# An encoder layer on one core: gates and RG-LRU projection in 2x2 blocks, products that run on in one PSUM bank, and a mix that is turned

## The chip, the core and the metric

The kernel runs on one core of a Trainium2 chip. A core has five engines that run side by side and meet at semaphores: TensorE (PE in the profile; its weight loads are shown apart as PEld), VectorE (DVE), ScalarE (ACT), GpSimd (POOL) and SyncE (SP), which here only issues transfers. TensorE writes its products into PSUM, 128 partitions of 8 banks of 512 fp32 numbers; DVE and ACT read them from there. Everything else lies in SBUF, and inputs, outputs and scratch lie in DRAM.

The metric is the time of one execution on the device in microseconds (us), lower is better. It is the median of several runs.

## What is computed

One layer of a hybrid encoder over 512 tokens of width 1024, in fp32:

```python
h = rmsnorm(x, mix_norm)
rx, ry, qkv, z, ba, gates = split(h @ w_in)          # w_in: 1024 x 9248
y_rnn = rglru_branch(rx, ry, ...) @ w_rnn_proj       # 1536 x 1024
y_dn  = deltanet_branch(qkv, z, ba, ...) @ w_dn_proj # 1024 x 1024
g_rnn, g_dn = split(sigmoid(gates))                  # 2 x 1024 columns
x = x + (g_rnn * y_rnn + g_dn * y_dn) @ w_out
gt, up = split(rmsnorm(x, ffn_norm) @ w_gate_up)     # 1024 x 2*2816
x = x + (silu(gt) * up) @ w_down
return rmsnorm(x, final_norm)
```

The RG-LRU branch is a short convolution, two gates and a linear scan along the tokens in both directions, times gelu(ry). The DeltaNet branch has 8 heads of 128 and works on chunks of tokens in both directions; its output is normalised per head and multiplied by silu(z).

## The kernel before

**Precision.** Each fp32 operand of a large product is split in two parts: hi, a copy rounded to the type that TensorE takes in one pass (a cast on ACT), and lo = value - hi (a subtraction on DVE, in a few places on POOL or by a DMA that accumulates). A product is hi*hi + hi*lo + lo*hi, three matmuls for each k-tile of 128.

**Two forms of product.** The plain form, `mm3`, keeps a weight tile of 128 output columns in TensorE and streams 512 tokens: the result has channels on the partitions. The block form (`products`, used for z; the same scheme by hand in gate/up, w_out and w_down) cuts tokens, rows and columns in halves and computes the 2x2 blocks with seven products in place of eight, from sums of blocks (names "1" to "7"). Sums of weight blocks are made by DMAs that add to what lies in SBUF (on POOL's queue, `accum_op`); sums of the normed input h are made once in `h_combos` and kept in DRAM (`xqd`).

**Stages.** Norm and transposes of x; four groups of three RG-LRU blocks (`rg_front` for rx, `rg_out` for ry); the z columns (`zset`); four groups of two DeltaNet heads (`dn_front`, `dn_mats`, `dn_inverse`, `dn_state`, `dn_out`); the gates, the RG-LRU projection (`rnn_part`) and the DeltaNet projection (`dn_part`); the mix times w_out; the second norm; gate/up, 22 tiles of 128 columns, of which 20 in block form; w_down; the last norm.

Before the change the gates and both projections are in the plain form. `rnn_part(i, n)` multiplies half of the 1536 rows by 128 columns; `rnn_gate(n)` and `dn_gate(n)` make 128 columns of a gate; `dn_part(h0, nh, n)` multiplies four heads by 128 columns and adds the gated result to the mix. The mix has channels on the partitions (`mixs`), as w_out's product needs it; `out_q(j)` makes the block sums of 256 of its columns.

**What sets the order.** The functions only record operations. `ORDER` lists all of them by number, over all engines; `Plan.emit` issues them in that order, and each engine works through its own queue in it. `HOMES` gives each SBUF and PSUM tile (pools t2, t4, ps) its place, and a new user of a place waits for the last user of it. All eight PSUM banks are places of this kind. Since every operation is issued through one recorder, all have the same line, L516, in the profile; they are told apart by the names of their tiles (t, ps, hh, hl, na and so on), engines and shapes.

Of the kernel before, what the change touches and what calls it, by code (L numbers as in the profile page):

```python
# [464 lines left out]
"""  # L465
LASTK = 3
DSPLIT = 4
GATES = (0, 2, 4, 6, 16)
RG_GROUPS = [[0, 1, 2], [3, 4, 5], [6, 7, 8], [9, 10, 11]]

# [51 lines left out]
def trunk(ctx: ExitStack, tc: tile.TileContext, x, mix_norm, w_in, rg_conv_w, rg_conv_b, rg_wa, rg_ba, rg_wx, rg_bx,  # L522
# [431 lines left out]


    mix = [None] * KD

    def k_proj(wv, n, k0, kts, acts):
        po = mmb()
        hi, lo = weights(wv[:, k0:k0 + kts, n * P:(n + 1) * P], kts)  # L960
# [964 lines left out]
```

## Time and profile before

| | us |
|---|---|
| median of 3 runs | 1039.06 |
| lowest and highest | 1038.81, 1039.10 |
| span of the profiled execution | 1038.7 |
| matmul instructions in it | 6675 |
| mean granted TensorE clock | 0.997 |
| HBM read and written | 133.18 MB, 18.91 MB |

The profile is of one execution. "Busy" is the time in which an engine had an instruction at work. Matmuls are pipelined, so a record lasts longer than the distance to the next start. The chain of work goes back from the last instruction, at each step to what released it. Rows of groups give the operation, its output and input tiles, partitions x elements, the count, busy us and mean ns of one, and then the idle time of the engine just before them with what ended it. Rows of stretches give the busy time of the engines asked for, with their counts, then the granted clock, the share of the 16 DMA engines' time and GB/s.

### The profile page before, as it was taken

How to read it: one execution, taken by the hardware profiler on the slowest of the kernel's cores; microseconds unless marked ns; L12 is line 12 of the kernel's file. 1: busy time of each engine (PE TensorE's matmuls, PEld its weight loads, DVE VectorE, ACT ScalarE, POOL GpSimd, SP SyncE). 2: the span in 40 equal slices, each digit the busy share in tenths (PEclk: the TensorE clock that was granted, in tenths of full speed). 3: DMA queues.
4: the chain of work that ended last, by engine and by line, in shares of the span. 5: the costliest groups of instructions: out<-in, count | busy, mean ns of one | idle time of the engine just before them, and what ended most of it. 6: DMA issues, size and time to landing. Idle time of an engine off the chain costs nothing.

```text
span 1038.7 us, 18051 instructions
## 1 busy us (share of the span) xinstructions
PE 1028.2 (99%) x6675; PEld 902.0 (87%) x6675; DVE 906.1 (87%) x1699; ACT 730.5 (70%) x1331; POOL 91.1 (9%) x145
## 2 busy tenths in 40 slices
PE   9999999999999999999999999999999999999997
PEld 8988888888888888798888888889999999998886
DVE  6899998959896589659859979999999998999998
ACT  8699999998457766798897565578444544455674
POOL 6000000112000111142212000000000000000000
PEclk9999999999999999999999999999999999999999
DMA  9952442325644125979985636976555332256532
GB/s 300 308 159 85 144 120 85 90 56 127 183 96 122 50 80 151 267 177 219 232 222 134 183 114 213 304 217 200 166 174 173 118 102 82 83 203 198 180 109 81
DMA packets 185512, 163.75 MB, mean 158 GB/s; under 512 B 7728, under 2 KB 156352, under 8 KB 185424
## 3 DMA queue, kind: packets, MB, share of 16 engines
q1 hardware_dynamic: 178752, 144.37, 46.0%
q0 software_dynamic: 5344, 14.82, 7.9%
q10 hardware_dynamic: 1328, 3.42, 0.9%
q8 instruction: 52, 0.85, 0.3%
q14 instruction: 36, 0.29, 0.1%
HBM read 133.18 MB, written 18.91 MB: 146 GB/s over the span
## 4 chain that ended last, share of the span: by engine, by line
PE 98%; ACT 1%; DMA 0%; issue 0%; DVE 0%; ACTq 0%; DVEq 0%
PE ps L516 98%; ACT t L516 1%; DMA t<-in_w_in_dram 0%; ACTq L516 0%; DVE t L516 0%; ACT L516 0%; DVE na L516 0%; DVEq L1920 0%; DVE so L516 0%; ACT so L516 0%; ACT rst L516 0%; ACT warm L516 0%; DVE rin L516 0%
## 5 line engine op out<-in xcount | busy, mean ns | idle before, releaser
L516 PE MATMUL ps<-t,t 128*128 128x512 f32 (+3 forms) x3039 | 536.0, 322 | 2.5 <-issue 1.6
L516 DVE TENSOR_TENSOR t<-t,t 128x512 fp32r<-128x512 f32 (+19 forms) x807 | 506.3, 658 | 27.8 <-ACT t L516 13.4
L516 PEld LDWEIGHTS ps<-t,t 128*128 128x128 f32 (+1 forms) x3039 | 430.6, 180 | 58.2 <-issue 2.7
L516 PE MATMUL ps<-hh,t 128*128 128x512 f32 (+2 forms) x1680 | 456.5, 347 | 0.0
L516 ACT CAST t<-t 128x512 fp32r<-128x512 f32 (+2 forms) x400 | 298.0, 780 | 158.9 <-DVE t L516 60.5
L516 PEld LDWEIGHTS ps<-hh,t 128*128 128x128 f32 (+1 forms) x1680 | 298.1, 189 | 38.2 <-ACT t L516 0.2
L516 PE MATMUL ps<-hl,t 128*128 128x512 f32 (+2 forms) x848 | 278.6, 347 | 0.0
L516 PEld LDWEIGHTS ps<-hl,t 128*128 128x128 f32 (+1 forms) x848 | 158.4, 189 | 19.5 <-issue 0.2
L516 ACT ACT_TABLE_LOAD x73 | 93.7, 1283 | 12.0 <-DVE so L516 5.1
L516 DVE SCALAR_TENSOR_TENSOR t<-ps,par,t 128x511 f32<-128x511 f32 (+1 forms) x108 | 79.3, 744 | 14.7 <-ACT t L516 13.7
L516 ACT COPY t<-ps 128x512 f32<-128x512 f32 (+3 forms) x108 | 44.3, 429 | 52.7 <-PE ps L516 51.4
L516 ACT ACTIVATE t<-t 128x128 f32<-128x128 f32 (+5 forms) x114 | 72.6, 647 | 9.8 <-DVE t L516 8.0
L516 DVE TENSOR_TENSOR t<-ps,t 128x256 f32<-128x256 f32 (+1 forms) x106 | 50.3, 486 | 11.4 <-PE ps L516 8.7
L516 DVE TENSOR_TENSOR t<-t 128x512 f32<-128x512 f32 (+1 forms) x81 | 51.0, 636 | 0.9 <-DMA t<-in_w_out_dram 0.6
L516 ACT ACTIVATE t<-ps,par 128x512 f32<-128x512 f32 x68 | 45.8, 707 | 7.4 <-PE ps L516 7.2
L516 POOL TENSOR_SCALAR_AFFINE_SELECT t<-t 128x512 f32<-128x512 f32 x32 | 25.6, 807 | 218.5 <-DMA t<-gcr 107.5
L516 PE MATMUL ps<-t,na 128*128 128x128 f32 (+2 forms) x640 | 42.9, 232 | 0.0
L516 PEld LDWEIGHTS ps<-t,na 128*128 128x128 f32 (+2 forms) x640 | 39.6, 145 | 3.8 <-issue 1.4
L516 ACT ACTIVATE t<-ps 128x512 f32<-128x512 f32 (+1 forms) x58 | 28.7, 508 | 15.5 <-PE ps L516 15.0
L516 PE MATMUL ps<-ident,t 128*128 128x128 f32 (+1 forms) x200 | 32.4, 276 | 0.3 <-DVE t L516 0.3
L516 POOL DMA_DIRECT2D t<-t x20 | 18.1, 938 | 146.4 <-ACT t L516 131.3
L516 DVE SCALAR_TENSOR_TENSOR t<-ps,negc,t 128x128 f32<-128x128 f32 x48 | 13.7, 344 | 19.0 <-PE ps L516 18.9
(151 smaller groups left out, 612.4 us busy)
## 6 DMA issues: line engine op xcount, KB each, us to landing
t<-in_w_in_dram SPq DMA_DIRECT2D x70, 512.0 KB, 5.2
t<-in_w_gate_up_dram SPq DMA_DIRECT2D x44, 512.0 KB, 5.0
t<-in_w_down_dram SPq DMA_DIRECT2D x22, 512.0 KB, 4.9
t<-t POOLq DMA_DIRECT2D x20, 512.0 KB, 6.0
t<-in_w_down_dram SPq DMA_DIRECT2D x33, 256.0 KB, 3.8
t<-in_w_out_dram SPq DMA_DIRECT2D x12, 512.0 KB, 6.0
t<-in_w_rnn_proj_dram SPq DMA_DIRECT2D x16, 384.0 KB, 3.6
sums<-t SPq DMA_DIRECT2D x11, 512.0 KB, 4.1
```

Source lines behind the costliest of these rows:

```text
L516: self.plan.ops.append((self.eng, {x.tensor.name for x in aps}, outs, lambda: real(*a, **kw)))
```

## The change

- The gates (two sets of 1024 columns) and the RG-LRU projection are now computed with tokens on the partitions, as 2x2 blocks with seven products (`merged`), in place of the plain form. A set has seven products of n blocks, n = 2 for the gates and 3 for the projection. For the gates the blocks of h come from `h_get2`; for the projection `mixed` makes them from the RG-LRU output, which is no longer split in hi and lo by `rg_out`.
- In `merged` several products run on in the same PSUM banks: bank pair bx takes products 6, 7, 4 (and 1 in the projection), bz takes 5 and 3, bw takes 2 (and 1 in the gates). The signs of some sums are turned for that. Between two products the sum so far is copied out.
- The DeltaNet projection has tokens on the partitions too (`dn_half`, four heads at a time, 512 columns), with the same number of matmuls as before.
- The mix is kept with tokens on the partitions (`mixt`) and turned by 32 transposes ahead of w_out, whose blocks are now taken in the order 2, 3, 0, 1.
- In gate/up the products 1, 6, 7, 4 run on in one bank and 5 and 3 in another, so that a tile takes three banks in place of four and two operations fewer on DVE, with two copies more on ACT.
- `WAYS` says for each product how its lo part is made: V on DVE, P on POOL, D by an accumulating DMA.
- `ORDER` and `HOMES` are made anew; ORDER has 9344 operations in place of 9257. In its new form the second gate set stands ahead of the RG-LRU projection, the first one behind it. Ahead of the last group's output transposes 20 matmuls of the DeltaNet projection stand behind the last state matmul (27 before). Of the last `dn_half`, 64 matmuls stand behind the point from which the last two heads are needed; then 29 transposes of the turn, then the first product with w_out.

```diff
-DSPLIT = 4
-GATES = (0, 2, 4, 6, 16)
+OUT_J = (2, 3, 0, 1)
+GATES = (0, 6, 12, 18, 28)
+WAYS = {"z": dict(zip("1234567", "PPDVVVD")), "r": dict(zip("1234567", "VVVVVVV")), "g": dict(zip("1234567", "VVDVVVD")),
+        "h": dict(zip("1234567", "VVDVVVD"))}
...
-        V.tensor_tensor(gy, h_, gy, ALU.mult)
-        y = four(F32R)
-        split(gy, y)
-        yr[b] = y
+        if b % 2 == 0:
+            yr[b // 2] = four()
+        V.tensor_tensor(yr[b // 2][:, b % 2, :], h_, gy, ALU.mult)
...
+    def block(wv, c0, rows, way, name, j, run):
...
+        if name == "1":
+            src = four()
+            for k in range(2):
+                Q.dma_start(src[:, k, :], part(0, 0)[:, k, :])
+        elif name in "237":
+            src = new(t4, (P, 2, 512), "t4", 1)
+            for k in range(2 if name == "2" else 1):
+                ks = slice(k, k + 1) if name == "2" else slice(0, 2)
+                Q.dma_start(src[:, ks, :], part(*{"2": (1, 0), "3": (1, 1), "7": (0, 1)}[name])[:, ks, :])
+            if name == "7":
+                G.dma_start(src, part(1, 1), accum_op=ALU.add)
+        else:
+            if name == "5":
+                run[j] = four()
+                Q.dma_start(run[j], part(0, 0))
+            src = run[j]
+            G.dma_start(src, part(*{"5": (0, 1), "6": (1, 1), "4": (1, 0)}[name]), accum_op=ALU.add)
+        hi, lo = four(F32R), four(F32R)
+        if way == "D":
+            A.copy(hi, src)
+            A.activation(lo, f(hi), AF.Copy, scale=-1.0)
+            G.dma_start(lo, src, accum_op=ALU.add)
...
+        else:
+            parts_of(src, hi, lo)
+        return hi, lo
+
+    def block_mm(po, w, x_, start, stop, add=False):
+        (hi, lo), (xh, xl) = w, x_
+        for i in range(2):
+            t_ = slice(i * P, (i + 1) * P)
+            for k in range(2):
+                T.matmul(po[i], xh[:, k, t_], hi[:, k, :], start=start and k == 0, stop=False, skip_group_check=add)
+                T.matmul(po[i], xh[:, k, t_], lo[:, k, :], start=False, stop=False, skip_group_check=add)
+            for k in range(2):
+                T.matmul(po[i], xl[:, k, t_], hi[:, k, :], start=False, stop=stop and k == 1, skip_group_check=add)
+
+    def merged(wv, c0, rows, n, ways, xs_, sink, apart):
+
+        run, bx, bz = {}, [mmb(), mmb()], [mmb(), mmb()]
+        bw = [mmb(), mmb()]
+        es, ms_, rs = ([two(), two()] for _ in range(3))
+        for name in "1256743":
+            po = bz if name in "53" else bw if name == "2" or apart and name == "1" else bx
+            add = name in ("2743" if apart else "6743")
+            for j in range(n):
+                w = block(wv, c0, rows, ways[name], name, j, run)
+                block_mm(po, w, xs_(name, j), j == 0 and not add, j == n - 1, add)
...
+            for i in range(2):
+                if name == "1":
+                    A.copy(es[i], po[i])
+                elif name == "2":
+                    if apart:
+                        sink(i, 0, po[i])
+                    else:
+                        sink(i, 0, po[i], es[i], ALU.add)
+                elif name in "67":
+                    d = {"6": ms_, "7": rs}[name][i]
+                    if apart:
+                        V.tensor_tensor(d, po[i], es[i], ALU.add)
+                    else:
+                        A.copy(d, po[i])
+                    if name == "7":
+                        sink(2 + i, 1, bz[i], rs[i], ALU.subtract)
...
+    def mixed(raw, n):
+
+        def get(name, j):
...
+                if name in "563":
+                    a_, b_, op = {"5": (x21, x22, ALU.subtract), "6": (x21, x11, ALU.subtract), "3": (x12, x11, ALU.add)}[name]
+                    V.tensor_tensor(q, a_, b_, op)
+            hi, lo = two(F32R, (P, 2, 256)), two(F32R, (P, 2, 256))
+            parts_of(q, hi, lo)
+            return hi, lo
...
+    def rnn_gate(c, n, src, other=None, op=None):
+        g = two()
+        if other is not None:
+            V.tensor_tensor(g, src, other, op)
+            src = g
+        act(g, src, AF.Sigmoid)
+        V.tensor_tensor(mixt[c][:, n, :], mixt[c][:, n, :], g, ALU.mult)
...
+    def dn_half(half):
+        ys = {}
+        for k in range(4 * half, 4 * half + 4):
+            ys[k] = four(F32R)
+            split(ydf[k // 2][:, k % 2, :], ys[k])
+        for n in range(2):
+            po = [mmb() for _ in range(NT)]
+            for j in range(2):
+                k0 = 4 * half + 2 * j
+                src, hi, lo = new(t4, (P, 2, 512), "t4", 1), four(F32R), four(F32R)
+                Q.dma_start(src, wd[:, k0:k0 + 2, 512 * n:512 * n + 512])
+                parts_of(src, hi, lo)
...
+            for c in range(NT):
+                if half == 0:
+                    A.copy(dnp[c][:, n, :], po[c])
+                else:
+                    t_ = dnp[c][:, n, :]
+                    V.tensor_tensor(t_, po[c], t_, ALU.add)
+                    V.tensor_tensor(t_, t_, gds[c][:, n, :], ALU.mult)
+                    V.tensor_tensor(mixt[c][:, n, :], mixt[c][:, n, :], t_, ALU.add)
...
+    rset = merged(wr, 0, lambda half, j: slice(6 * half + 2 * j, 6 * half + 2 * j + 2), 3, WAYS["r"], mixed(yr, 3), rnn_sink, False)
+    steps(rset, 22)
+    g1set = merged(win, C_G, halves_h, 2, WAYS["g"], h_get2, rnn_gate, True)
+    g2set = merged(win, C_G + D, halves_h, 2, WAYS["h"], h_get2, dn_gate, True)
...
-    for n in range(KD):
-        dn_part(DSPLIT, H - DSPLIT, n)
-        if n % 2:
-            out_q(n // 2)
+    for j in OUT_J:
+        for h in range(2):
+            n = 2 * j + h
+            pt = axb()
+            for c in range(NT):
+                turn(pt[:, c * P:(c + 1) * P], mixt[c][:, n // 4, n % 4 * P:(n % 4 + 1) * P])
+            A.copy(mixs[j][:, h, :], pt)
+        out_q(j)
...
-        A_, B_, C_, D_ = (mmb(), stb(), axb(), axb() if n % 2 else mmb())
+        X_, W_, Z_ = mmb(), stb(), axb()
...
+        product(px, w7["1"], xs7["1"], True)
+        A.copy(e[:, 0, :], px)
+        product(pw, w7["2"], xs7["2"], True)
+        V.tensor_tensor(s_[:, lo_], pw, e[:, 0, :], ALU.add)
+        act(s_[:, lo_], s_[:, lo_], AF.Silu)
+        product(px, w7["6"], xs7["6"], False)
+        A.copy(e[:, 1, :], px)
+        product(pz, w7["5"], xs7["5"], True)
+        product(px, w7["7"], xs7["7"], False)
+        A.copy(e[:, 0, :], px)
+        V.tensor_tensor(u[:, hi_], pz, e[:, 0, :], ALU.subtract)
+        product(px, w7["4"], xs7["4"], False)
+        act(s_[:, hi_], px, AF.Silu)
+        product(pz, w7["3"], xs7["3"], False)
+        V.tensor_tensor(u[:, lo_], pz, e[:, 1, :], ALU.subtract)
```

More of the change, by code (lines that the diff above doesn't have):

```diff
@@ L901, in trunk @@
     wx = rg_wx[0].rearrange("d n k j -> k n d j")
-    yr = [None] * NB
+    yr = [None] * (NB // 2)
     def rg_front(b):
@@ L953, in rg_mid @@
         return [rg_rest(b, r, i, t) for b, (r, i), t in zip(bs, fr, th)]
[L956 to L960, printed above, removed]
-        mm3(po, hi, lo, lambda k: acts[k0 + k][:, 0, :], lambda k: acts[k0 + k][:, 1, :], kts)
-        return po
     kq = {}
-    ktok, vn, osum, ydn = {}, {}, {}, [None] * H
+    ktok, vn, osum = {}, {}, {}
     rn, n2, nq = {}, {}, {}
@@ L1241, in trunk @@
     wd = w_dn_proj[0].rearrange("(k p) n -> p k n", p=P)
-    mixs = [four() for _ in range(4)]
-    gds = [four() for _ in range(4)]
-    def rnn_part(i, n):
-        po = k_proj(wr, n, 6 * i, 6, yr)
-        m_ = mixs[n // 2][:, n % 2, :]
-        if i == 0:
-            A.copy(m_, po)
-        else:
-            V.tensor_tensor(m_, m_, po, ALU.add)
-    def rnn_gate(n):
-        g = two()
-        po = in_proj(C_G + n * P)
-        act(g, po, AF.Sigmoid)
-        m_ = mixs[n // 2][:, n % 2, :]
-        V.tensor_tensor(m_, m_, g, ALU.mult)
@@ L1260, in products, with part @@
-    def products(wv, c0, rows, n, by_dma, xs_, sink, rins):
+    mixt = [four() for _ in range(NT)]
+    gds = [four() for _ in range(NT)]
+    def block(wv, c0, rows, way, name, j, run):
+        def part(half, col):
+            return wv[:, rows(half, j), c0 + 512 * col:c0 + 512 * col + 512]
+        if name == "1":
[9 more added lines that the diff above has]
+                G.dma_start(src, part(1, 1), accum_op=ALU.add)
+        else:
+            if name == "5":
[8 more added lines that the diff above has]
+            G.dma_start(lo, src, accum_op=ALU.add)
+        elif way == "P":
+            for k in range(2):
+                A.copy(hi[:, k, :], src[:, k, :])
+                G.tensor_tensor(lo[:, k, :], src[:, k, :], f(hi[:, k, :]), ALU.subtract)
+        else:
+            parts_of(src, hi, lo)
+        return hi, lo
@@ new lines, in block_mm @@
+    def block_mm(po, w, x_, start, stop, add=False):
[5 more added lines that the diff above has]
+                T.matmul(po[i], xh[:, k, t_], lo[:, k, :], start=False, stop=False, skip_group_check=add)
+            for k in range(2):
+                T.matmul(po[i], xl[:, k, t_], hi[:, k, :], start=False, stop=stop and k == 1, skip_group_check=add)
@@ L1262, in products @@
+    def products(wv, c0, rows, n, ways, xs_, sink, rins):
         m, w, v, run = four(), four(), four(), {}
@@ L1269, in products @@
             for j in range(n):
-                def part(half, col):
-                    return wv[:, rows(half, j), c0 + 512 * col:c0 + 512 * col + 512]
-                if name == "1":
-                    src = four()
-                    for k in range(2):
-                        Q.dma_start(src[:, k, :], part(0, 0)[:, k, :])
-                elif name in "237":
-                    src = new(t4, (P, 2, 512), "t4", 1)
-                    for k in range(2 if name == "2" else 1):
-                        ks = slice(k, k + 1) if name == "2" else slice(0, 2)
-                        Q.dma_start(src[:, ks, :], part(*{"2": (1, 0), "3": (1, 1), "7": (0, 1)}[name])[:, ks, :])
-                    if name == "7":
-                        G.dma_start(src, part(1, 1), accum_op=ALU.add)
-                else:
-                    if name == "5":
-                        run[j] = four()
-                        Q.dma_start(run[j], part(0, 0))
-                    src = run[j]
-                    G.dma_start(src, part(*{"5": (0, 1), "6": (1, 1), "4": (1, 0)}[name]), accum_op=ALU.add)
@@ L1291, in products @@
-                if j % 2:
-                    hi, lo = four(F32R), four(F32R)
-                else:
-                    hi, lo = new(t4, (P, 2, 512), "t4", 1, F32R), new(t4, (P, 2, 512), "t4", 1, F32R)
-                if name in by_dma:
-                    A.copy(hi, src)
-                    A.activation(lo, f(hi), AF.Copy, scale=-1.0)
-                    G.dma_start(lo, src, accum_op=ALU.add)
-                elif name in "12":
-                    for k in range(2):
-                        A.copy(hi[:, k, :], src[:, k, :])
-                        G.tensor_tensor(lo[:, k, :], src[:, k, :], f(hi[:, k, :]), ALU.subtract)
-                else:
-                    parts_of(src, hi, lo)
@@ L1305, in products @@
-                xh, xl = xs_(name, j)
-                first, last = j == 0, j == n - 1
-                for i in range(2):
-                    t_ = slice(i * P, (i + 1) * P)
-                    for k in range(2):
-                        T.matmul(po[i], xh[:, k, t_], hi[:, k, :], start=first and k == 0, stop=False)
-                        T.matmul(po[i], xh[:, k, t_], lo[:, k, :], start=False, stop=False)
-                    for k in range(2):
-                        T.matmul(po[i], xl[:, k, t_], hi[:, k, :], start=False, stop=last and k == 1)
+                hi, lo = block(wv, c0, rows, ways[name], name, j, run)
@@ L1314, in products @@
+                last = j == n - 1
+                block_mm(po, (hi, lo), xs_(name, j), j == 0, last)
                 if not last:
@@ L1347, in h_get, with h_get2 @@
         return parts
+    def h_get2(name, j):
+        if name in "124":
+            k, t = (0, 4, 4)["124".index(name)] + 2 * j, 256 * (name == "4")
+            return hh[:, k:k + 2, t:t + 256], hl[:, k:k + 2, t:t + 256]
+        return h_get(name, j)
+    def mixed(raw, n):
+        def get(name, j):
+            lo_, hi_ = raw[j], raw[n + j]
+            x11, x21, x12, x22 = lo_[:, :, 0:256], lo_[:, :, 256:512], hi_[:, :, 0:256], hi_[:, :, 256:512]
+            if name == "7":
+                q = two(shape=(P, 2, 256))
+                V.scalar_tensor_tensor(q, x11, -1.0, x22, ALU.mult, ALU.subtract)
+            else:
+                q = {"1": x11, "2": x12, "4": x22, "5": x21, "6": x11, "3": x12}[name]
+                if name in "563":
[4 more added lines that the diff above has]
+            return hi, lo
+        return get
     def h_combos():
@@ L1357, in h_combos @@
             x11, x12, x21, x22 = raw[0, 0], raw[0, 1], raw[1, 0], raw[1, 1]
-            for name, q, a_, b_ in (("5", x22, x21, x22), ("7", x21, x11, x21), ("6", x11, x11, x22), ("3", x12, x12, x11)):
-                V.tensor_tensor(q, a_, b_, ALU.subtract)
+            for name, q, a_, b_, op in (("5", x22, x21, x22, ALU.subtract), ("7", x21, x11, x21, ALU.subtract),
+                                        ("6", x11, x22, x11, ALU.subtract), ("3", x12, x12, x11, ALU.add)):
+                V.tensor_tensor(q, a_, b_, op)
                 hi, lo = two(F32R, (P, 2, 256)), two(F32R, (P, 2, 256))
@@ L1379, in steps, with rnn_sink @@
                 break
-    def dn_gate(n):
-        po = in_proj(C_G + D + n * P)
-        act(gds[n // 2][:, n % 2, :], po, AF.Sigmoid)
-    def dn_part(h0, nh, n):
-        po = k_proj(wd, n, h0, nh, ydn)
-        m_ = mixs[n // 2][:, n % 2, :]
-        t_ = two()
-        V.tensor_tensor(t_, po, gds[n // 2][:, n % 2, :], ALU.mult)
-        V.tensor_tensor(m_, m_, t_, ALU.add)
-    def dn_split(h):
-        ydn[h] = four(F32R)
-        split(ydf[h // 2][:, h % 2, :], ydn[h])
+    def rnn_sink(c, n, src, other=None, op=None):
+        if other is None:
+            A.copy(mixt[c][:, n, :], src)
+        else:
+            V.tensor_tensor(mixt[c][:, n, :], src, other, op)
@@ new lines, in rnn_gate, with dn_gate @@
+    def rnn_gate(c, n, src, other=None, op=None):
[5 more added lines that the diff above has]
+        V.tensor_tensor(mixt[c][:, n, :], mixt[c][:, n, :], g, ALU.mult)
+    def dn_gate(c, n, src, other=None, op=None):
+        g = gds[c][:, n, :]
+        if other is not None:
+            V.tensor_tensor(g, src, other, op)
+            src = g
+        act(g, src, AF.Sigmoid)
+    def dn_half(half):
[11 more added lines that the diff above has]
+                for c in range(NT):
+                    t_ = slice(c * P, (c + 1) * P)
+                    for k in range(2):
+                        T.matmul(po[c], ys[k0 + k][:, 0, t_], hi[:, k, :], start=j == 0 and k == 0, stop=False)
+                        T.matmul(po[c], ys[k0 + k][:, 0, t_], lo[:, k, :], start=False, stop=False)
+                    for k in range(2):
+                        T.matmul(po[c], ys[k0 + k][:, 1, t_], hi[:, k, :], start=False, stop=j == 1 and k == 1)
+            for c in range(NT):
+                if half == 0:
+                    A.copy(dnp[c][:, n, :], po[c])
+                else:
+                    t_ = dnp[c][:, n, :]
+                    V.tensor_tensor(t_, po[c], t_, ALU.add)
+                    V.tensor_tensor(t_, t_, gds[c][:, n, :], ALU.mult)
+                    V.tensor_tensor(mixt[c][:, n, :], mixt[c][:, n, :], t_, ALU.add)
@@ L1413, in trunk @@
     halves_h = lambda half, j: slice(4 * half + 2 * j, 4 * half + 2 * j + 2)
-    zset = products(win, C_Z, halves_h, 2, "37", h_get, store_sink(zs, AF.Silu), rin01)
+    zset = products(win, C_Z, halves_h, 2, WAYS["z"], h_get, store_sink(zs, AF.Silu), rin01)
     rest = []
@@ L1421, in trunk @@
             dn_front(0)
-        if done < 6 and bs[0] >= 6:
-            for n in range(KD):
-                rnn_part(0, n)
-            done = 6
     rg_flush()
-    for n in range(KD):
-        rnn_part(1, n)
     steps(zset, 15)
+    rset = merged(wr, 0, lambda half, j: slice(6 * half + 2 * j, 6 * half + 2 * j + 2), 3, WAYS["r"], mixed(yr, 3), rnn_sink, False)
+    steps(rset, 22)
+    g1set = merged(win, C_G, halves_h, 2, WAYS["g"], h_get2, rnn_gate, True)
+    g2set = merged(win, C_G + D, halves_h, 2, WAYS["h"], h_get2, dn_gate, True)
     wdn = w_down[0].rearrange("(j h p) n -> p j h n", p=P, h=2)
@@ L1458, in out_sums @@
         Q.dma_start(osums[j][:, 1], rb)
-    gates = [(rnn_gate, n) for n in range(KD)] + [(dn_gate, n) for n in range(KD)]
+    gates = [g1set] * 14 + [g2set] * 14
+    dnp = None
     for g in range(4):
@@ L1467, in trunk @@
             dn_front(g + 1)
-        for fn, n in gates[GATES[g]:GATES[g + 1]]:
-            fn(n)
+        for st_ in gates[GATES[g]:GATES[g + 1]]:
+            steps(st_, 1)
         if g == 1:
@@ L1472, in trunk @@
                 out_sums(j)
-    for h in range(DSPLIT):
-        dn_split(h)
-    for n in range(KD):
-        dn_part(0, DSPLIT, n)
-    for h in range(DSPLIT, H):
-        dn_split(h)
+            dnp = [four() for _ in range(NT)]
+            dn_half(0)
+        if g == 2:
+            steps(g1set, 14)
+            steps(g2set, 14)
+    dn_half(1)
+    mixs = [four() for _ in range(4)]
     xq = {}
@@ L1499, in out_q2 @@
         xq[j].update({"3": p3, "2": p2, "4": p4})
-    for n in range(KD):
-        dn_part(DSPLIT, H - DSPLIT, n)
-        if n % 2:
-            out_q(n // 2)
+    for j in OUT_J:
+        for h in range(2):
+            n = 2 * j + h
+            pt = axb()
+            for c in range(NT):
+                turn(pt[:, c * P:(c + 1) * P], mixt[c][:, n // 4, n % 4 * P:(n % 4 + 1) * P])
+            A.copy(mixs[j][:, h, :], pt)
+        out_q(j)
     xall = new(dn, (P, NT, D), "na", 1)
@@ L1564, in trunk @@
     ob = {"6": [stb(), stb()], "7": [axb(), axb()], "5": [axb(), mmb()], "1": [mmb(), mmb()]}
-    for j in range(nj):
+    for j in OUT_J:
         w4 = out_w(j)
@@ L1568, in trunk @@
             for i in range(2):
[L1569 removed]
+                half_mm(ob[name][i], i, w4[name], xq[j][name], j == OUT_J[0], j == OUT_J[-1])
         out_q2(j)
@@ L1660, in trunk @@
     qs = {}
-    for name, q, x_, y_ in (("5", q5, a21, a22), ("7", q7, a11, a21), ("6", q6, a11, q5), ("3", q3, a12, q6)):
-        V.tensor_tensor(q, x_, y_, ALU.subtract)
+    for name, q, x_, y_, op in (("5", q5, a21, a22, ALU.subtract), ("7", q7, a11, a21, ALU.subtract), ("6", q6, q5, a11, ALU.subtract), ("3", q3, a12, q6, ALU.add)):
+        V.tensor_tensor(q, x_, y_, op)
         qh, ql = four(F32R, (P, 4, 256)), four(F32R, (P, 4, 256))
```

30 lines of the change are left out of this document (11 added, 19 removed), and 869 rows, old and new, of tables (HOMES, ORDER).

## The prediction

> **What bounds the kernel now.** I read the head of the profile's page first, then the chain that ended last, then the waits of the matmul engine alone, and last the stages.
>
> ```profile
> span 1038.7 us, 18051 instructions
> PE 1028.2 (99%) x6675; PEld 902.0 (87%) x6675; DVE 906.1 (87%) x1699; ACT 730.5 (70%) x1331; POOL 91.1 (9%) x145
> PE 98%; ACT 1%; DMA 0%; issue 0%; DVE 0%; ACTq 0%; DVEq 0%
> 9.03 417.90 PE ps L516 x2289
> 428.53 197.78 PE ps L516 x1534
> 633.00 398.49 PE ps L516 x2665
> PE ps L516 <- issue: 1.6, 1, 1.6
> PE ps L516 <- POOL ones L516: 1.1, 1, 1.1
> PE ps L516 <- ACT t L516: 0.9, 1, 0.9
> PE ps L516 <- DVE t L516: 0.3, 1, 0.3
> ```
>
> The chain is TensorE (PE) from 9.03 to 1031.49 us, with two short breaks, and PE idles 3.9 us in the whole span. So the time is the sum of PE's work plus 9.0 us ahead and 7.2 us behind. There is almost no stall to win back: what a change gives is the PE work it takes away, and what it costs is PE work and every wait that it puts in front of PE.
>
> **What one PE instruction costs.** A matmul's recorded length includes its pipeline, so it must not be summed. What counts is the distance from start to start.
>
> ```profile
> L516 PE MATMUL ps<-t,t 128*128 128x512 f32 x266 | 60.5, 389 | 0.0
> 633.00 0.76 PE L516 MATMUL ps<-ident,t 128*128 128x128 f32 x4 [0.32 <-DVE t L516]
> 633.52 0.95 PE L516 MATMUL ps<-t,t 128*128 128x512 f32 x3
> 634.30 0.62 PE L516 MATMUL ps<-ident,t 128*128 128x128 f32 x4
> L516 PE MATMUL ps<-ident,t 128*128 128x128 f32 x194 | 31.7, 278 | 0.3 <-DVE t L516 0.3
> 850.00:900.00 50.00, 50.00 (x419) 1.00 0.29 81
> ```
>
> The first row is the stretch 940 to 1000 us (count, busy us, mean ns), 512 columns only: 60.5/266 = 0.227 us each, though one lasts 389 ns. In 850 to 900 us (PE busy and count, granted clock, DMA share, GB/s), 256 columns only, it is 50/419 = 0.119 us. Four transposes through the identity take 633.52 - 633.00 = 0.52, or 0.130 us each.
>
> **The sum on PE.** Gates: before, 16 projections of 8 k-tiles x 3 = 384 matmuls; after, 2 sets x 7 products x 2 blocks x 12 = 336. RG-LRU projection: 16 x 6 x 3 = 288 before; 7 x 3 x 12 = 252 after. DeltaNet projection: 192 both times. All have 512 columns, so 84 go: 84 x 0.227 = 19.1 us. Turning the mix adds 8 x 4 = 32 transposes: 32 x 0.130 = 4.2 us; the three short gaps in such a run give less, so 3.0 is the lower end, and I take 3.5. Gate/up keeps its 84 matmuls of 256 columns a tile. Work alone: 1038.7 - 19.1 + 3.5 = 1023.1 us.
>
> [...]
>
> **The other engines.** Durations for DVE (VectorE) and ACT (ScalarE):
>
> ```profile
> L516 DVE TENSOR_TENSOR t<-t,t 128x512 fp32r<-128x512 f32 x224 | 149.5, 687 | 3.8 <-ACT t L516 2.8 <-issue 0.4
> L516 DVE TENSOR_TENSOR t<-t,t 128x1024 fp32r<-128x1024 f32 x116 | 141.0, 1223 | 2.8 <-PE ps L516 2.4 <-issue 0.2
> L516 DVE TENSOR_TENSOR t<-t,t 128x768 fp32r<-128x768 f32 x31 | 29.2, 954 | 10.0 <-ACT t L516 7.3 <-PE ps L516 2.7
> L516 DVE TENSOR_TENSOR t<-ps,t 128x256 f32<-128x256 f32 x80 | 32.6, 421 | 9.5 <-PE ps L516 6.8 <-ACT t L516 2.1
> L516 ACT CAST t<-t 128x512 fp32r<-128x512 f32 x232 | 137.7, 618 | 88.3 <-DVE t L516 46.2 <-PE ps L516 28.1 <-DMA t<-in_w_dn_proj_dram 8.5
> L516 ACT COPY t<-ps 128x512 f32<-128x512 f32 x44 | 25.2, 583 | 14.8 <-PE ps L516 14.4
> L516 ACT COPY t<-ps 128x256 f32<-128x256 f32 x22 | 8.2, 373 | 27.6 <-PE ps L516 26.8 <-DVE t L516 0.8
> 700.00:800.00 100.00, 100.00 (x834) 99.86 (x833) 97.37 (x168) 56.51 (x106) 0.00 (x0) 1.00 0.59 183
> ```
>
> DVE loses the low parts of 16 RG-LRU weight tiles (16 x 0.954), of 12 outputs, 16 DeltaNet weight tiles and 8 heads (36 x 0.687), of 4 gate tiles (4 x 1.223), 48 sums and products (48 x 0.687), and in gate/up 2 x 0.421 for each of 20 tiles: 94.7 us. It gains 49 low parts of weight blocks (49 x 1.223) and 99 operations of 512 columns (33 on RG-LRU operands, 6 and 28 in the sinks, 32 in the DeltaNet halves; 99 x 0.687): 128 us. Net +33, so 939 us in some 1025, 92%. The last row has DVE at 97.4% with PE unbroken, so I cost this at nothing; the cover is DVE's run ahead of PE, and where that ends, at the tail, I count separately. ACT gains some 15 us in gate/up (2 x 0.373 x 20) and some 30 elsewhere at 70% busy: nothing.
>
> Products that run on in one bank make PE wait until it is emptied: 0.373 us on ACT in gate/up, or 0.421 on DVE. In the new order at least 7 other matmuls (7 x 0.119 = 0.83 us) stand between such a pair, so nothing; uncovered, the three emptyings by ACT would cost 3 x 20 x 0.373 = 22 us. In the gate sets the two row halves alternate: 6 matmuls (1.36 us) against 0.687.
>
> **Two new waits.** First, the last group's output. Before, this chain ran from the last state matmul to the transposes:
>
> ```profile
> 626.31 0.02 issue
> 626.33 0.55 DVE t L516 x3
> 626.88 0.06 issue
> ...
> 632.51 0.36 DVE t L516
> 632.87 0.14 issue
> ```
>
> That is 6.7 us up to 633.00, under 27 matmuls of the DeltaNet projection (6.1 us); only 0.32 us of PE idled. In the new order 20 stand there (4.5 us). Some of the adds of the chain come earlier now, so the wait is between 0 and 2.2 us; I take 1.5.
>
> Second, the turn. Before, each pair of output columns was finished, mixed and used while the next was multiplied. Now a whole half must be mixed before it can be turned. The matmuls that need the last two heads, and 16 that stand among them, take PE 64 x 0.227 = 14.5 us. DVE starts on them 1.6 us in and has 24 operations, 16.5 us, of which the first half to be turned ends at about 15; two copies (0.583), the subtraction (0.687, behind other mix work) and the cast (0.618) put the first output product at about 19.1. PE has 29 transposes until about 17.7. Over the whole tail DVE needs 1.6 + 16.5 + 0.7 + 9.9 (out_q) + 7.3 (out_w) + 5.5 (out_q2) = 41.5 us and PE 14.5 + 3.6 + 96 x 0.227 = 39.9, so the wait is about 2: 0 at best, 5 if DVE also idles. I take 2.
>
> Behind it PE runs as before. The new tables move every other operation too: there is no more than the 3.9 us of idle time to win by that, and I set a loss at nothing, with the longest break shown (1.6 us) as its other end. Sum: 1023.1 + 1.5 + 2.0 = 1026.6 of span; the median of the runs is 0.4 over the profiled span, so **1027.0 us**.
>
> **The rivals.** (a) *DMA becomes the bound*, the case that is slower than before. A block costs one load per product, and four of the seven accumulate in flight (POOL's queue), as do the low parts of two in the gates; the sets also reload their mixed operands.
>
> ```profile
> q1 hardware_dynamic: 178752, 144.37, 46.0%
> q0 software_dynamic: 5344, 14.82, 7.9%
> 0.00:50.00 50.00, 35.92 (x77) 1.00 1.04 304
> 450.00:500.00 50.00, 41.38 (x106) 1.00 0.91 221
> 312.00:400.00 88.00, 63.42 (x135) 1.00 0.34 97
> ```
>
> The last three rows give DVE busy, granted clock, DMA share and GB/s of a stretch. From the first two a megabyte takes 0.460 x 1038.7/144.37 = 3.31 us of all 16 engines on SP's queue, and 0.079 x 1038.7/14.82 = 5.54 on POOL's. Down the new order, from 312 to 520 us of PE work, stand 94 transfers of SP (35.6 MB) and 31 accumulating ones (16.2 MB): 118 + 90 = 208 us of DMA in 208 us of PE, where before it was 72 and 19, 150 us. If DMA keeps up no more than the 0.91 of 450 to 500 us, this takes 228 us: +20, 1047. The case turns slower than before below 208/(208 + 14) = 0.94. For it: accumulations wait on one another through one buffer. Against it: the 1.04 of the first 50 us, and 0.91 was a demand, not a limit, since PE did not idle. A part of it (+6 to +10, 1033 to 1037) is as likely as the whole.
>
> (b) *Nothing waits*: the order hides both chains, as the old one hid its own: 1023.1 + 0.4 = 1023.5.
>
> (c) *DVE's tail costs more*: if each of the 24 evacuations also loses a 0.2 us handover, +5: 1032.
>
> (d) *Transposes go at their full length*, 32 x 0.278 = 8.9: +5.4, 1032. The rows at 633 us speak against it. [...]
>
> **How the numbers follow.** Forecast 1027 (1025 to 1031) 0.58; (b) 0.12; (c) 0.07; (d) 0.03; (a) 0.20, of which 0.04 still faster, 0.06 level, 0.10 slower. A measurement of this kernel tells about 0.2%, 2 us, from no change. So faster 0.84, same 0.06, slower 0.10. The range, 1022.5 to 1038, holds the bounds of the transposes and of both waits and the milder half of (a), and leaves out about 0.1 above.
>
> **What would show it.** PE's matmul count lower by 84 and its transposes up by 32, PE about 15 us less busy; the chain still PE at 97% or more; a break of 1 to 2 us ahead of the last group's transposes and of 1 to 4 us ahead of the first output product, both released by DVE or ACT. DMA share near 1 between 300 and 520 us with PE unbroken says that (a) is wrong; breaks of PE there that end on weights of w_in or w_rnn_proj say that it is right, and the prediction with it wrong. Breaks inside gate/up would mean that the bank is emptied late.

## The result, and the profile after

| | before | after |
|---|---|---|
| median, us | 1039.10 (5 runs) | 1128.36 (5 runs, 1126.83 to 1131.04) |
| ratio after/before | | 1.0854, 95% interval 1.0840 to 1.0867 |
| span of the profiled execution, us | 1038.7 | 1129.3 |
| matmul instructions | 6675 | 6623 |
| TensorE idle, us (span less busy) | 10.5 | 60.7 |
| mean granted TensorE clock | 0.997 | 0.975 |

The change is 89 us slower, where 12 faster was forecast and 1038 was the upper end. The experiments give medians of four runs; the median of the kernel before, run again beside each, lay between 1039.1 and 1040.6 us, so 1 or 2 us from one experiment to another say nothing. One run of the closer filling in experiment 5 took 5817.87 us and is not counted with its other three (1071.5 to 1074.4), and the profiled run of experiment 2 took 1090.17 us, where its other three took 1083.

The head and the chain of the page after:

```profile
span 1129.3 us, 18175 instructions
PE 1068.6 (95%) x6623; PEld 913.1 (81%) x6623; DVE 956.8 (85%) x1707; ACT 764.9 (68%) x1397; POOL 118.8 (11%) x165
PE 72%; DVE 12%; ACT 10%; issue 3%; DMA 2%; SPq 0%; ACTq 0%; DVEq 0%
```

The count is as forecast: 52 fewer, 84 matmuls less and 32 transposes more. But the chain, 98% PE before, now goes through DVE and ACT for 22%, and PE is *busy* 40 us longer with less work: a busy row also holds time in which matmuls start late (after the change late starts sum to 119.7 us, as shown below, where PE idles 60.7) and time at half clock (55 us of the span after, 6 before).

The waits of PE in the same trace (total us, times, longest), and stretches of 100 us (busy time of PE, its weight loads, DVE, ACT, POOL; then clock, DMA share, GB/s), the first two of the kernel before, the others of the changed one:

```profile
PE ps L525 <- DVE t L525: 31.2, 52, 2.9
PE ps L525 <- ACT t L525: 7.4, 14, 1.0
PE ps L525 <- DVE na L525: 4.3, 4, 2.3
PE ps L525 <- ACT na L525: 3.7, 3, 1.5
```

```profile
0.00:100.00 100.00, 97.99 (x519) 84.62 (x520) 83.08 (x151) 85.28 (x139) 17.73 (x29) 1.00 0.74 221
500.00:600.00 100.00, 100.00 (x894) 85.10 (x893) 82.21 (x235) 79.65 (x179) 16.18 (x29) 1.00 0.72 182
```

```profile
0.00:100.00 100.00, 90.28 (x458) 76.41 (x459) 80.69 (x142) 81.64 (x134) 17.19 (x29) 0.95 0.68 196
200.00:300.00 100.00, 99.16 (x440) 80.47 (x438) 82.19 (x146) 77.13 (x113) 19.45 (x22) 1.00 0.79 195
400.00:500.00 100.00, 93.03 (x632) 75.22 (x633) 78.14 (x170) 68.62 (x143) 25.57 (x38) 0.97 0.88 232
500.00:600.00 100.00, 89.88 (x609) 73.21 (x607) 76.79 (x187) 77.36 (x171) 20.60 (x31) 0.90 0.63 156
600.00:700.00 100.00, 87.98 (x651) 72.28 (x651) 70.82 (x191) 56.82 (x124) 8.39 (x18) 0.95 0.38 103
900.00:1000.00 100.00, 99.31 (x818) 98.25 (x818) 91.85 (x154) 53.59 (x114) 0.00 (x0) 1.00 0.48 145
```

Most of the loss lies between 340 and 740 us, where the DeltaNet heads run, and a smaller part in the first 50 us, where x is normed and transposed; gate/up is nearly whole. DVE is the releaser, yet it is only 71% busy from 600 to 700, where PE loses most: its operations come late there, they are not too many.

To place the loss I took, for every matmul, the distance to the next start less the normal distance of its form (0.227 us for 512 columns, 0.119 for 256, 0.11 for 128 and for transposes). This sums to 13.7 us before and 119.7 after. Of the 106 between them about 13 come in the first 50 us and most of the rest from 340 to 740. By the function of the matmul that came late: `dn_state` 0.4 before, 51.2 after; `dn_inverse` 2.6 and 18.5; outside any named stage (most of it at the start) 3.6 and 14.3; `products` 2.4 and 6.3; `dn_front` 2.1 and 5.5; `dn_mats` 0 and 5.0; `merged` 0 and 4.3; gate/up 0 and 3.7. The functions of the DeltaNet heads are not touched by the change; their place in ORDER is.

The state after, on the timeline (start, duration, engine, operation; in brackets the idle time before it and its releaser):

```profile
693.02 0.49 PE L525 MATMUL ps<-t,t 128*128 128x128 f32 x2 [0.54 <-DVE t L525]
693.55 0.35 DVE L525 SCALAR_TENSOR_TENSOR t<-t,ge,ps 128x128 f32<-128x128 f32 x1 [0.58 <-PE ps L525]
693.95 0.49 PE L525 MATMUL ps<-t,t 128*128 128x128 f32 x2 [0.44 <-DVE t L525]
...
696.72 0.49 PE L525 MATMUL ps<-t,t 128*128 128x128 f32 x2 [0.22 <-DVE t L525]
697.24 0.35 DVE L525 SCALAR_TENSOR_TENSOR t<-ps,negc,t 128x128 f32<-128x128 f32 x1 [0.58 <-PE ps L525]
697.65 0.49 PE L525 MATMUL ps<-t,t 128*128 128x128 f32 x2 [0.44 <-DVE t L525]
```

and before, the step whose reads take `negc` (the lower three rows above):

```profile
609.69 1.06 PE L516 MATMUL ps<-t,t 128*128 128x128 f32 x8
610.50 1.40 PE L516 MATMUL ps<-hh,t 128*128 128x512 f32 x5
610.79 1.13 DVE L516 SCALAR_TENSOR_TENSOR t<-ps,negc,t 128x128 f32<-128x128 f32 x4 [1.22 <-PE ps L516]
611.74 1.05 PE L516 MATMUL ps<-t,na 128*128 128x128 f32 x8
```

Before, four chains are multiplied in a row (x8: two passes each), five other matmuls follow, and in their cover DVE makes its four reads. After, one chain is multiplied, DVE reads it, and only then the next is multiplied, though they share nothing but the PSUM bank: 693.95 - 693.02 and 697.65 - 696.72 are both 0.93 us, for one slice. PE and DVE each wait for the other.

ORDER shows how often. In 143 places of the new one a matmul that writes a bank stands behind a read of another part of this bank, though the functions record it ahead (95 in `dn_state`, 25 in `dn_inverse`); in the old one there is none. The wait for the read is there though the two touch different columns: the matmul at 693.95, with 0.44 us of idle time put down to DVE before it, writes columns 256 to 383 of its bank, takes nothing that the read at 693.55 makes, and that read takes columns 0 to 127. What asks for such a wait is not shown; the trace shows that it stands there, and its price: 0.93 us for a slice in place of some 0.2 (two passes, 0.11 us apart, in the row at 609.69).

### The profile page after: what moved, and what is told of

Same layout as the page of the kernel before. It is cut to its first block, busy times and chain, and to the rows that moved or that the text cites. A ratio compares the mean times of both kernels' runs of the same rounds, so it can differ in the third digit from the quotient of the medians.

```text
span 1129.3 us, 18175 instructions
## 1 busy us (share of the span) xinstructions
PE 1068.6 (95%) x6623; PEld 913.1 (81%) x6623; DVE 956.8 (85%) x1707; ACT 764.9 (68%) x1397; POOL 118.8 (11%) x165
## 3 DMA queue, kind: packets, MB, share of 16 engines
q10 hardware_dynamic: 1328, 3.42, 0.8%
## 4 chain that ended last, share of the span: by engine, by line
PE 72%; DVE 12%; ACT 10%; issue 3%; DMA 2%; SPq 0%; ACTq 0%; DVEq 0%
PE ps L525 72%; DVE t L525 11%; ACT t L525 7%; ACT L525 1%; DVE na L525 1%; DMA osums<-t 1%; DMA t<-in_w_in_dram 1%; ACT na L525 0%; DMA sums<-t 0%; ACT ps L525 0%; DMA t<-in_w_gate_up_dram 0%; ACT hh L525 0%; ACT rst L525 0%; SPq L525 0%; ACTq L525 0%
## 5 line engine op out<-in xcount | busy, mean ns | idle before, releaser
L525 PE MATMUL ps<-t,t 128*128 128x512 f32 (+3 forms) x3195 | 599.4, 334 | 27.5 <-DVE t L525 20.2
L525 DVE TENSOR_TENSOR t<-t,t 128x512 fp32r<-128x512 f32 (+15 forms) x839 | 553.0, 686 | 58.5 <-ACT t L525 28.2
L525 PEld LDWEIGHTS ps<-t,t 128*128 128x128 f32 (+1 forms) x3195 | 465.1, 182 | 106.4 <-DVE t L525 32.9
L525 PE MATMUL ps<-hh,t 128*128 128x512 f32 (+2 forms) x1424 | 375.8, 341 | 0.8 <-DVE na L525 0.8
L525 PEld LDWEIGHTS ps<-hh,t 128*128 128x128 f32 (+1 forms) x1424 | 249.6, 190 | 32.4 <-ACT t L525 2.0
L525 PE MATMUL ps<-hl,t 128*128 128x512 f32 (+2 forms) x720 | 232.7, 340 | 0.0
L525 ACT COPY t<-ps 128x256 f32<-128x256 f32 (+3 forms) x168 | 70.1, 434 | 92.4 <-PE ps L525 84.9
L525 ACT ACTIVATE t<-t 128x512 f32<-128x512 f32 (+5 forms) x118 | 72.1, 618 | 12.9 <-DVE t L525 12.2
L525 PE MATMUL ps<-ident,t 128*128 128x128 f32 (+2 forms) x232 | 44.5, 284 | 10.6 <-DVE t L525 3.9
L525 PEld LDWEIGHTS ps<-ident,t 128*128 128x128 f32 (+2 forms) x232 | 30.1, 146 | 19.9 <-DVE t L525 5.7
```

Source lines behind the costliest of these rows:

```text
L525: self.plan.ops.append((self.eng, {x.tensor.name for x in aps}, outs, lambda: real(*a, **kw)))
```

## The experiments

The ORDER of a kernel is a list of numbers, so an edit of it is shown as one place of many.

**1. Writes ahead of reads.** The first theory was that the turns in a bank are the whole loss.

```diff
-3425(PE) 3429(DVE) 3423(PE) 3427(DVE) 3426(PE) 3430(DVE) 1909(PE) 3424(PE) 3428(DVE)
+3425(PE) 3423(PE) 3426(PE) 1909(PE) 3424(PE) 3429(DVE) 3427(DVE) 3430(DVE) 3428(DVE)
```

> The changed kernel, whole computation, with one thing altered in ORDER: in 143 places a TensorE operation that writes one slice of a PSUM bank stood behind a DVE or ACT read of another slice of that bank, though the program records all writes ahead of the reads; here the writes go first again (read moved behind them), nothing else is moved. Theory (write and read take turns in a bank, each waits for the other): in the profile the gap in front of these 143 is 70.5 us of PE time, and some 49 us on other operations are in part its consequence (late chains, clock at half). So 1128 - 70 to 1128 - 100: 1030 to 1058 us. Rival 'the block form with its DMAs or the run-on of products in a bank costs the time': those are untouched, 1110 or more. Rival 'too little other work stands between the steps of the DeltaNet state': the steps stay where they are, 1100 or more.

> The same, only in the DeltaNet state (95 of the 143 places). Theory: 36.9 us of gaps directly, with its part of the 49 at most 63: 1065 to 1091 us. Rivals (DMA, block form, too little other work between the steps): 1120 to 1130.

> The same, in the 48 other places only (inverse, front, matrices and the first transposes); the state is left as it is. Theory: 22 us of gaps directly, with its part of the 49 at most 40: 1088 to 1108 us, and its gain and that of the state alone add up to about that of all. Rivals: 1120 to 1130.

Measured: all 1093.32 us (ratio to before 1.0515, interval 1.0497 to 1.0532), the state alone 1106.06, the rest alone 1114.25. The gains of the two parts, 22.3 and 14.1, add up to about the 35.0 of all, so the two sets of places hardly overlap, and the turns cost time. But only half as much came back as the gaps had promised: all three runs fall between the ranges of the theory and of the rivals, and 53 us over the kernel before were left.

**2. The turns put into the kernel before.**

```diff
-3356(PE) 3357(PE) 3358(PE) 3359(PE) ... 3360(DVE) 3362(DVE) 3361(DVE) 3363(DVE)
+3356(PE) ... 3360(DVE) 3357(PE) 3361(DVE) 3358(PE) 3362(DVE) 3359(PE) 3363(DVE)
```

> The kernel before, whole computation, nothing of the change in it: only in its ORDER the four matmuls into one bank and the four DVE reads of it, in five steps... of the DeltaNet state (three banks of reads for the right side, two for the new state, in each of four groups), stand alternately: matmul, read, matmul, read. 60 such turns. Theory: 36.9/95 = 0.39 us a turn directly, 23 us, and up to twice that with what follows: 1059 to 1084 us. Rivals (DMA, block form): no change, 1037 to 1041.

Measured: 1082.93 us against 1040.56 (1.0428, 1.0393 to 1.0462), so 42.4/60 = 0.71 us a turn, near the upper end of the theory's range. Nothing of the change is in this kernel. The 0.71 us hold more than the turn: in the profiled run TensorE worked 31 us at half clock (3 before), and with three of the four matmuls moved behind other work, 20 of the 64 ways counted in experiment 5 have under 1.1 us of cover (5 before). PE's waits in it; before, the first row read 0.3 us, once:

```profile
PE ps L516 <- DVE t L516: 21.9, 52, 0.7
PE ps L516 <- ACT t L516: 1.8, 3, 0.9
```

**3. The DMAs, rival (a) of the prediction.** One of the three places that are edited alike:

```diff
-G.dma_start(src, part(1, 1), accum_op=ALU.add)
+G.dma_start(src[:, 0, 0:128], part(1, 1)[:, 0, 0:128], accum_op=ALU.add)
```

> The changed kernel with the writes of each bank ahead of its reads (as in the run of all 143), and of its accumulating DMAs in the block products (sums of weight blocks and low parts, 25 MB on POOL's queue) only one column in eight is moved; sums are then wrong in the other columns. Every operation, wait and place stays. Theory (what is left of the loss is the order of the queues): 1080 to 1095 us against 1093 with all the bytes. Rival (a) of the prediction (the DMAs bound the stages from 312 to 520 us): 1060 us or less.

Measured: 1087.85 us, 5.5 less than with all bytes. The stretch from 425 to 475 us, with all bytes (first) and with an eighth:

```profile
425.00:475.00 50.00, 45.48 (x366) 36.25 (x364) 35.53 (x89) 35.57 (x65) 10.55 (x12) 0.95 0.92 232
```

```profile
425.00:475.00 50.00, 45.45 (x394) 36.03 (x393) 36.18 (x89) 34.54 (x67) 10.05 (x13) 0.97 0.51 146
```

The DMA share falls from 0.92 to 0.51, and PE is busy 45.5 us in both; by the distances from start to start it does 44 us of work with all bytes and 45 with an eighth. A DMA share near 1 was no bound here. The plain loads on SP's queue were left as they are; for these there is the trace of the changed kernel, where from 300 to 520 us DVE waits 0.9 us and ACT 1.9 for a DMA, and PE not at all.

**4. ORDER written anew by mean durations.** This was to show that the loss is all in the order.

```diff
-ORDER: as given
+ORDER: each engine, when free, takes the first operation of the old ORDER
+       whose inputs and place are there by the mean durations
```

> The changed kernel, whole computation, same operations, same HOMES: only ORDER is written anew. It is made by letting each engine, whenever it comes free, take the first operation of the old ORDER that has its inputs and its place by then, with the mean durations of the rows of the profiles, and with all writes of a PSUM bank ahead of the reads of it. Theory (the whole loss lies in the order: turns in a bank, and operations that stand at the head of a queue and wait while others behind them are ready): the forecast's sum, 1027, up to 1045 us. Rivals (accumulating DMAs as the bound, block form or run-on of products in a bank dear by themselves): these are all still there, 1085 us or more.

> The kernel before, whole computation, its ORDER written anew in the same way. TensorE idles 3.9 us in it, so there is little to win: 1030 to 1045 us. With the run above it compares the two forms of the computation at orders of one make: theory, the changed form is level or up to 15 us faster; rivals, it is 40 us or more slower.

Measured: the changed kernel 1113.55 us, the kernel before 1079.64 (1.0382, 1.0365 to 1.0399). The first came out in the range of its rivals (1085 or more), the second outside its only range, and the comparison of the two forms (34 us apart) lies between theory and rival. Since the same way of writing ORDER makes the kernel before slower too, the first result is no evidence for the rivals. What the pair does show: an order that is nearly free of waits on mean durations cost the kernel before 39 us with not one operation changed. In its trace single breaks are long:

```profile
PE ps L516 <- ACT t L516: 14.2, 12, 4.5
PE ps L516 <- DVE t L516: 9.9, 6, 4.4
```

That an order without slack fails on every operation that comes later than planned is the likely reason, but no run here shows it. The pair does not say what a good order would give.

**5. Cover.** The second theory: TensorE stands at the head of its queue before a short chain through DVE or ACT, and nothing is put between. On each of the 64 ways of the state from one group of four matmuls through its readers to the next group I summed the PE work that ORDER puts between. In the kernel before it is never under 0.9 us, and under 1.1 on 5 ways; in the changed one it is under 1.1 on 25, and on 12 of these about 0.2 or less; writing first (experiment 1) leaves these counts as they are. Filling changes TensorE's queue alone:

```diff
-3424 3433 3431 3759 1873 3432 3434
+3424 3759 1873 3433 3431 3432 3434
```

(3759 and 1873 are matmuls of `dn_front` and `products`, the others of the state.)

> The changed kernel with the writes of each bank ahead of its reads (1093 us as measured), and TensorE's own queue changed: 213 matmuls and transposes whose operands had by the profile's durations been there for at least 1 us stand earlier, in front of one that would wait over 0.3 us. The order on DVE, ACT, POOL and SP, the operations and HOMES are untouched; whole computation. Theory (what is left of the loss is TensorE standing at the head of its queue before a short chain through DVE or ACT, with nothing put between): most of the 50 us of gaps at full clock goes, 1045 to 1065 us. Rivals (DMAs, or DVE and ACT as the bound): filling the gaps only moves them, 1085 us or more.

> The changed kernel with its turns in a bank left as they are (143 places), and only TensorE's own queue filled as in the run of 213: operations ready for 1 us stand ahead of one that would wait over 0.3 us. Whole computation. If turns in a bank and missing cover are two separate losses: 1128 less about the 21 us that the filling gave behind the regrouping, 1100 to 1112 us. If a turn costs only where nothing stands in it (one loss, the wait at the head of the queue): 1070 to 1095 us, near the run with both.

> The changed kernel, writes ahead of reads, and TensorE's queue filled more closely: an operation that has been ready for 0.3 us goes ahead of one that would wait over 0.05 us. Whole computation. If cover is all that is missing: 1050 to 1065 us, under the 1072 of the coarser filling. If TensorE's queue alone can't mend it, since buffers and the queues of DVE, ACT and SP are laid out for another course: 1068 to 1075 us.

| | reads between the writes | writes first |
|---|---|---|
| queue as given | 1128.36 | 1093.32 |
| PE's queue filled | 1095.44 | 1072.49 |
| filled more closely | | 1073.51 |

Each cure alone gives 33 to 35 us, both together 55.9, not 68: 12 us are won by either. They can be the same waits, which a filled queue hides and regrouped writes avoid, or the same half clock: TensorE works 51 us at half clock after the change, 21 with writes first, none with the queue filled alone and 3 with both. In the changed kernel matmuls of 512 columns start 0.427 us apart at half clock, 0.227 at full. Since a stretch at half clock so loses at most half its length, an estimate from these figures is that up to 15 of the 35 us, and up to 26 of the 33, are won through the clock; the runs do not tell these apart from the waits themselves. Filling behind the regrouping ended at 1072, between its range and that of its rivals; filling alone at 1095.4, just above the range for one loss. Closer filling gives nothing more, as the second of its two expectations had it. By the count of ways, filling behind the regrouping leaves 29 under 1.1 us but only one at 0.2 or less. So it is the bare ways that it covers; that these alone cost the time is not shown.

Of the 93 late starts of 0.25 us or more that PE has from 340 to 740 us in the changed kernel (62 us), nearly every one had a matmul among the next 400 of PE's queue whose operands were there and whose bank was free; with the queue filled 34 are left (19 us), and for about 10 of these there was none. PE's waits in the filled kernel, where the first row read 31.2 us after the change and the second 7.4:

```profile
PE ps L524 <- DVE t L524: 9.3, 17, 2.2
PE ps L524 <- ACT t L524: 3.2, 10, 0.7
```

**6. Cover taken from the kernel before.** Again only TensorE's queue.

```diff
-3359 2175 2176 2173 5064 5065 5066 3364
+2175 2176 2173 5064 5065 5066 ... 3359 3728 3729 3730 3731 3364
```

> The kernel before, whole computation, nothing of the change in it; of its ORDER only TensorE's own queue is changed. In it at least 0.9 us of other TensorE work stands on each of the 64 ways of the DeltaNet state from one group of four matmuls through DVE or ACT to the next. Here 196 matmuls and transposes that stood on such a way are put in front of its first group, so that 24 of the 64 ways have less than 1.1 us of cover, as 25 have in the changed kernel (5 before). Theory (TensorE waits at the head of its queue where a short chain has no cover): 24 ways lose 0.5 to 1.5 us each, 1052 to 1075 us. Rivals (only turns in a bank, or the DMAs, or the block form, cost time): 1037 to 1043 us.

Measured: 1067.22 us against 1040.53 (1.0261, 1.0243 to 1.0278), inside the theory's range. The clock has no part in this: TensorE works 3 us at half clock in both kernels. With 196 matmuls moved by a few places, PE waits for ACT and DVE 20 times, where before it waited twice:

```profile
PE ps L516 <- ACT t L516: 9.4, 10, 2.0
PE ps L516 <- DVE t L516: 9.1, 10, 1.6
```

**7. What holds the rest: DVE's load, or the other queues?**

```diff
-            parts_of(src, hi, lo)
+            A.copy(hi, src)
+            V.tensor_tensor(lo[:, 0, :], src[:, 0, :], f(hi)[:, 0, :], ALU.subtract)
...
-                T.matmul(po[i], xh[:, k, t_], lo[:, k, :], start=False, stop=False, skip_group_check=add)
+                T.matmul(po[i], xh[:, k, t_], lo[:, 0, :], start=False, stop=False, skip_group_check=add)
```

> The changed kernel as in the run with 213 filled places (1072 us). Of the low part of each weight block of the gates, the RG-LRU projection and six blocks of z that is made on DVE, only the first half is made (47 subtractions of 512 columns in place of 1024: about 25 us less on DVE, half of what the change added); the second k-tile's matmul takes the first half too, so the low parts are wrong there. TensorE's work, the waits and the order stay. Theory (DVE's load costs nothing, as predicted; its chains are late, not its throughput): 1067 to 1075 us. Rival (DVE is what is short): 1060 us or less.

> The same done on TensorE, DVE and ACT (operations ready for 0.6 us go ahead of one that would wait over 0.3 us); whole computation. Theory: a little less than the run with TensorE alone, 1040 to 1060 us, since DVE and ACT too stand at the head of their queues (ACT waited 50 us for TensorE and 15 for DVE from 365 to 690 us). If the waits of DVE and ACT cost nothing, level with that run.

> The changed kernel, whole computation, writes ahead of reads, and the queues of TensorE (345 operations), DVE (96), ACT (118) and SP (30) filled together: an operation that has been ready for 0.7 us goes ahead of one that would wait over 0.2 us; some groups of operations also start up to 300 places earlier or later in ORDER. If the order on the other queues holds the rest: 1045 to 1062 us. If the places in HOMES and the chains themselves hold it: 1068 to 1076 us, level with TensorE's queue alone.

Measured: with 25 us less on DVE (927.6 us busy against 952.3) 1068.34 us, 4.2 less than 1072.49 and inside the theory's range (3 to 4 less by the ratios to the kernel before, 1.0279 and 1.0314); with DVE and ACT filled too 1072.81, level; with four queues filled 1084.45, worse by 12, outside both ranges. DVE's load is worth a few microseconds, as is that of the DMAs. Operations put ahead on DVE and ACT do not help. The last run also shifts groups of operations in ORDER, so what harmed it stays open.

## Why the prediction was wrong

- **The sum on PE was right.** Count and form were as read, and the median distance of the matmuls of 512 columns is 0.227 us in both traces; the normal distances sum to 15.6 us less (19.1 less 3.5 forecast). The row of the turn, 29 transposes in the 3.45 us up to 744.02, gives 0.119 us each with a wait of 0.3 among them, not their length of 0.278, so rival (d) falls. The granted clock is 1.00 in the 3.45 us and in the 3.98 us behind them.

```profile
722.59 0.66 PE L525 MATMUL ps<-ident,t 128*128 128x128 f32 x4 [0.24 <-DVE t L525]
...
740.57 3.68 PE L525 MATMUL ps<-ident,t 128*128 128x128 f32 x29
744.02 0.47 PE L525 MATMUL ps<-t,t 128*128 128x512 f32 x1
```

- **The two new waits** were smaller than taken, inside their bounds: 0.4 us before the last group's output (1.5 taken, 0 to 2.2), 0.3 at the turn (2.0 taken, 0 to 5). PE came to both some 90 us later than before the change, so DVE had more time to run ahead than the forecast gave it. Rival (c) did not show.
- **DVE and ACT at no cost:** nearly. DVE rose to 957 us (939 forecast), and half of the added load was worth 3 to 4 us in the filled kernel.
- **Products that run on in one bank at no cost:** nearly. The late starts in gate/up sum to 3.7 us, where they were 0.0; the uncovered 22 us did not come.
- **Rival (a), the DMAs:** no. PE did break between 300 and 520 us, as the prediction had said it would if DMA were the bound, but on DVE and ACT; taking away seven eighths of the accumulated bytes gave 5.5 us.
- **The step that failed** is the last term of the sum: "The new tables move every other operation too: there is no more than the 3.9 us of idle time to win by that, and I set a loss at nothing, with the longest break shown (1.6 us) as its other end." What was set at nothing there measured 106 us of late starts (119.7 less 13.7), more than all other terms together. The bound was wrong in kind: breaks in the old trace tell how well the *old* order hides its chains. Covers of single waits were counted in the new ORDER where the change had put a new wait; in the DeltaNet heads, whose code is unchanged, none was counted. There ORDER itself shows both faults, the turns (120 of the 143 are in `dn_state` and `dn_inverse`) and the ways without cover. The first 50 us, with 13 of the 106, have no term of their own in the sum either; 4 of the 143 turns are in the transposes of x there.

What the runs show of the 106: 35 us go with the turns, or 33 with filled queue, and 56 with both. Some 6 go with the accumulating bytes and 3 to 4 with DVE's load, each measured on a repaired kernel. The best repaired kernel with all of the computation, 1072.49 us, is still 32 us slower than the kernel before (ratio 1.0314, 1.0299 to 1.0330). In its trace `dn_state` still comes 16.5 us late and `dn_inverse` 9.7. That the rest lies in the places of HOMES and in the courses of the other queues, which were laid out for another timing, is argued and not shown: HOMES was not tried anew. So whether the changed form, at an order as good as the old one, would reach 1027 stays open; no run here is faster than the kernel before.

## What to carry to other kernels

When a change replaces a hand-made order, the order is the change: count in the new one, for the untouched stages too, how much work stands on each short chain between engines, and whether writes and reads of one PSUM bank alternate. Slices of one bank written by TensorE and read by another engine belong in groups, all writes and then all reads, with at least a chain's length of other matmuls behind them (here 0.9 us sufficed, and a turn between write and read cost 0.71 us in experiment 2, with what followed from it). Here the idle time in the old profile bounded what a new order could win, and said nothing of what it could lose.

## What the hardware showed that was not expected

A break cost more than itself where the granted clock fell to 0.50 behind it. The kernel before has one break of 1.6 us, at 427 to 428.5 us; the four stretches of 3.41 us around it (clock third from the end):

```profile
421.73:425.14 3.41, 3.41 (x78) 2.63 (x77) 3.38 (x5) 3.30 (x8) 1.34 (x3) 1.00 1.10 260
425.14:428.56 3.42, 1.82 (x74) 1.41 (x73) 3.35 (x6) 2.61 (x6) 1.21 (x3) 1.00 1.09 243
428.56:431.97 3.41, 3.41 (x42) 2.77 (x43) 3.38 (x8) 2.62 (x8) 0.00 (x0) 0.50 1.12 249
431.97:435.38 3.41, 3.41 (x51) 2.58 (x51) 0.18 (x1) 1.84 (x5) 0.00 (x0) 1.00 1.00 295
```

The stretch behind the one with the break runs at half clock, though PE was busy for 1.82 of 3.42 us in it. That was not always so: in the changed kernel PE is busy for 1.61 of the 3.41 us from 411.76 to 415.17, 21 such stretches ahead of the fall of its clock at 483.44 us, with one break of 1.8 us, and the 3.42 us behind run at full clock. So the share of busy time alone does not decide, and what does is not shown. Of the whole span 55 us ran at half clock in the changed kernel, 23 in the one with writes first, 5 in the filled one and 6 in the kernel before.
